# Recutting the column tiles of a decoder trunk, and alternating two PSUM sets in its short convolution

## The chip, the cores and the metric

One Trainium2 chip, all 8 NeuronCores, each with a share of the tokens and all of the weights. The metric is the device time of the slowest core in microseconds (us). A die is four cores (0 to 3, 4 to 7).

The program has two states. In the fast one all cores show the same mean granted TensorE clock and runs agree within 0.3%. In the slow one the cores of one die, or of both, show a lower clock and take longer. A run is called undisturbed below when no die shows a lowered clock.

Words used below: TensorE multiplies a weight block by the columns of the other, the moving operand, and leaves its sums in PSUM; ScalarE and VectorE read PSUM and work on the tiles in SBUF. In the lines of the profile, PE is TensorE and PEld its weight loads, DVE is VectorE, ACT is ScalarE, POOL and SP issue the transfers. L317 is a line of the kernel, x48 a number of instructions, and [1.76 <-DVE ...] the idle time before them and what ended it. A line of the chain or of a timeline begins with start and length in us; a line by windows gives the window, its length, the busy times of PE, PEld, DVE, ACT and POOL (with the number of instructions), the granted clock, the DMA share and GB/s.

## The reference, cut to what matters

A two-layer trunk on a prompt group and a sample group. Each core holds 1024 prompt tokens, 16 sample tokens and, for what has to look back, 128 tokens before its prompt half.

```python
for i in range(2):
    h = h + 0.5 * swiglu(rmsnorm(h), ffn1)      # 2048 -> 5632 -> 2048
    a = rmsnorm(h)
    m = chunk_gmlp(a) if i == 0 else short_conv(a)
    h = h + m
    h = h + 0.5 * swiglu(rmsnorm(h), ffn2)
    h = h + sigmoid(rmsnorm(h) @ w_gate) * (p[i] @ w_proj)
y = rmsnorm(h)

# short_conv: bg, cg, xh = split(a @ w_in, 3);  ci = cg * xh
#             co[t] = w0*ci[t-2] + w1*ci[t-1] + w2*ci[t];  (bg * co) @ w_out
```

The first feed-forward and the v half of the gMLP need all 128 + 1024 + 16 = 1168 columns (tokens). After that the convolution needs only the last two of the 128 tokens before: 2 + 1024 + 16 = 1042 columns.

## The kernel before

Tokens lie along the free dimension: `h`, `xn` and `buf2` are [128, 16, 1168]. A row of `xn` (bf16) is 2336 bytes. The 1024 main columns came first, then the 128 earlier ones, then the 16 samples, so the 1042 needed ones were 0 to 1023 and 1150 to 1167.

```python
TT_FULL = [(0, 512), (512, 512), (1024, 144)]   # (first column, columns)
TT      = [(0, 512), (512, 512), (1150, 18)]

def mm_group(ws, wres, nk, rhs_fn, tts, pset, pres, reads):
    for k in range(nk):                          # weight blocks 128 x 128
        for ti, (t0, tn) in enumerate(tts):      # column tiles, one PSUM bank each
            matmul(pset[ti][:, 0:tn], lhsT=ws[:, k, :], rhs=xn[:, k, t0:t0+tn], ...)
```

Every stage calls `mm_group` for one output chunk after another, into the PSUM sets `PA` and `PB` (three banks each). One weight block is three matmuls; a group with 16 blocks is 48. Weights come in by six slots of 512 KB.

Between stages stands a normalisation:

```python
for (t0, tn) in tts:
    for c in range(16):
        ScalarE: sq[c % 2] = h[:, c, tile] ** 2
        TensorE: pst += ones.T @ sq[c % 2]
    ScalarE: rt = sqrt(pst / D + eps);  VectorE: rstd = 1 / rt
    for c in range(16):
        VectorE: xn[:, c, tile] = h[:, c, tile] * gain[c] * rstd
```

The convolution does three groups for each of its 16 chunks:

```python
for c in range(16):
    group -> PA;  ScalarE: cgs = PA              # cg
    group -> PB;  VectorE: ci = PB * cgs, then co from ci   # xh
    group -> PA;  VectorE: buf2[:, c] = PA * co  # bg
```

Of the kernel before, what the change touches and what calls it, by code (L numbers as in the profile page):

```python
# [6 lines left out]
F32 = mybir.dt.float32  # L7
F32R = mybir.dt.float32r
BF16 = mybir.dt.bfloat16
AF = mybir.ActivationFunctionType  # L10
# [10 lines left out]
TT_FULL = [(0, 512), (512, 512), (1024, 144)]  # L21
TT = [(0, 512), (512, 512), (1150, 18)]
# [102 lines left out]
def build_program():  # L125
# [73 lines left out]
    def sbt(name, shape, dt):  # L199
        uid[0] += 1  # L200
        return nc.sbuf_tensor("%s_u%d" % (name, uid[0]), shape, dt)
# [5 lines left out]
    with contextlib.ExitStack() as es:  # L207
# [70 lines left out]
        with contextlib.ExitStack() as ms:  # L278
# [131 lines left out]
            def ple(l, tts):  # L410
                with contextlib.ExitStack() as ps_:
                    pT = ps_.enter_context(sbt("pT", [128, 2, TH], BF16))
                    pblocks = [(j * 128, 128, j * 128) for j in range(8)] + [(1150, 18, 1150)]
# [36 lines left out]
            def gmlp():  # L450
                rmsnorm(G_MIX + 0, TT_FULL)
                with contextlib.ExitStack() as gs:
# [28 lines left out]
                    for c in range(NCH):  # L481
# [4 lines left out]
                        def emit_v(c=c, pset=pset):  # L486
                            nc.scalar.activation(out=buf2[:, c, 0:512], in_=pset[0][:, 0:512], func=AF.Gelu_apprx_tanh)
                            nc.scalar.activation(out=buf2[:, c, 512:1024], in_=pset[1][:, 0:512], func=AF.Gelu_apprx_tanh)
                            nc.scalar.activation(out=buf2[:, c, 1024:1152], in_=pset[2][:, 0:128], func=AF.Gelu_apprx_tanh)
                            return nc.scalar.activation(out=vsf[:, c, 0:16], in_=pset[2][:, 128:144], func=AF.Gelu_apprx_tanh)  # L490
# [147 lines left out]
            def sconv():  # L638
                rmsnorm(G_MIX + 1, TT)
                with contextlib.ExitStack() as cs:  # L640
# [7 lines left out]
                    co = C(sbt("co", [128, 1024], F32))  # L648
                    cit = C(sbt("cit", [128, NCH, 18], F32))
                    cos = C(sbt("cos", [128, 16], F32))  # L650
                    for c in range(NCH):
                        w0, w1, w2 = gcol(G_WC, c), gcol(G_WC + 1, c), gcol(G_WC + 2, c)
                        ws, wres = wget("c_in", 0, 0, 16, D + c * 128)
                        mm_group(ws, wres, 16, xn_rhs, TT, PA, "psA", XN_ALL)

                        def emit_cg():
                            last = None
                            for ti, (t0, tn) in enumerate(TT):
                                last = nc.scalar.activation(out=cgs[:, t0:t0 + tn], in_=PA[ti][:, 0:tn], func=AF.Copy)
                            return last  # L660
                        S.op("act", ["psA"], ["cgs"], emit_cg)
                        ws, wres = wget("c_in", 0, 0, 16, 2 * D + c * 128)
                        mm_group(ws, wres, 16, xn_rhs, TT, PB, "psB", XN_ALL)
                        cb = cib[c % 2]

                        def emit_ci(cb=cb, c=c):
                            nc.vector.tensor_tensor(out=cb[:, 2:514], in0=PB[0][:, 0:512], in1=cgs[:, 0:512], op=ALU.mult)
                            nc.vector.tensor_tensor(out=cb[:, 514:1026], in0=PB[1][:, 0:512], in1=cgs[:, 512:1024], op=ALU.mult)
                            nc.vector.tensor_tensor(out=cb[:, 0:2], in0=PB[2][:, 0:2], in1=cgs[:, 1150:1152], op=ALU.mult)
                            return nc.vector.tensor_tensor(out=cit[:, c, 2:18], in0=PB[2][:, 2:18], in1=cgs[:, 1152:1168],  # L670
                                                           op=ALU.mult)
                        S.op("dve", ["psB", "cgs"], [("cib", c % 2), ("cit", c)], emit_ci)

                        S.op("dve", [("cib", c % 2)], [("cit", c)], lambda cb=cb, c=c: nc.vector.tensor_copy(
                            out=cit[:, c, 0:2], in_=cb[:, 1024:1026]))
                        S.op("dve", [("cib", c % 2)], ["co"], lambda cb=cb, w0=w0: nc.vector.tensor_scalar(
                            out=co[:], in0=cb[:, 0:1024], scalar1=w0, scalar2=None, op0=ALU.mult))
# [189 lines left out]
```

## Time and profile before

| | before |
|---|---|
| five times before the prediction | 5913, 5916, 6540, 6639, 6785 us (median 6540) |
| profiled run | fast; cores 5907.1 to 5914.6 us, clock 0.939 to 0.941 |
| one weight block, 1168 columns | 494.1 ns (7.91 us a group) |
| one weight block, 1042 columns | 457.1 ns (7.31 us a group) |
| convolution, chunk to chunk | 23.84 us |
| normalisation, first square to first matmul | 46.95 us |

Divide a group's length by its 16 blocks: that is the number that the change is about. The lines themselves are in the prediction.

### The profile page before, as it was taken

The numbers are of one execution on the slowest core, as the hardware profiler recorded it, in microseconds if no ns is written. First come the engines' busy times: TensorE is split into PE (matmuls) and PEld (weight loads), VectorE is DVE, ScalarE is ACT, GpSimd is POOL, SyncE is SP. The second block draws the span as 40 slices with busy tenths as digits, with TensorE's granted clock in tenths as the row PEclk, the third lists the DMA queues.
The fourth block names the chain that finished last, engine by engine and source line by source line (L and its number), as shares of the span: only waits on it lengthen the run. The fifth ranks groups of instructions, "written<-read, shape, count | busy, mean of one in ns | idle before, by whom it ended". The sixth has DMA issues, their size and how long they took to land.

```text
span 5914.6 us, 78413 instructions; the slowest of 8 cores (5907.1 to 5914.6 us)
## 1 busy us (share of the span) xinstructions
PE 5398.7 (91%) x33572; PEld 2668.8 (45%) x33572; DVE 1205.3 (20%) x2549; ACT 542.9 (9%) x1286; POOL 811.3 (14%) x724
## 2 busy tenths in 40 slices
PE   5999999975698999999779999997999899999976
PEld 3555555533344444444334444443444444444434
DVE  3111010124312110101330101113321201010135
ACT  2000000020102000000220000001000200000020
POOL 0111111100011111111111111110111111111110
PEclk7999999976798999999789999997999899999978
DMA  4777777743375777776457787874777577878734
GB/s 90 66 65 68 66 67 67 65 43 29 37 72 48 71 75 72 72 72 66 40 52 73 71 73 70 73 71 46 67 66 65 47 72 72 73 71 72 68 40 93
DMA packets 1405253, 382.73 MB, mean 65 GB/s; under 512 B 1398838, under 2 KB 1402330, under 8 KB 1402526
## 3 DMA queue, kind: packets, MB, share of 16 engines
q0 software_dynamic: 1395968, 354.46, 66.3%
q1 hardware_dynamic: 8942, 23.24, 1.2%
q8 instruction: 270, 4.42, 0.3%
q14 instruction: 73, 0.60, 0.0%
HBM read 723.28 MB, written 8.93 MB: 124 GB/s over the span
## 4 chain that ended last, share of the span: by engine, by line
PE 88%; DVE 7%; ACT 2%; DMA 2%; issue 2%; DVEq 0%; ACTq 0%; SPq 0%
PE pa_u L317 46%; PE pb_u L317 39%; DVE xn_u L350 3%; PE pst_u L340 1%; ACT sq_u L337 1%; DVE rstd_u L347 1%; DMA x_tok_u<-xin 1%; ACT sig_u L426 1%; DVE buf_u L551 1%; DVE st_u L515 0%; DVE fst_u L763 0%; DVE yo_u L777 0%; DMA p_tok_u<-pin 0%; PE x_pt_u L257 0%; DVE vhb_u L528 0%
## 5 line engine op out<-in xcount | busy, mean ns | idle before, releaser
L317 PE MATMUL pa_u<-xn_u,wsl_u 128*128 128x512 bf16 (+2 forms) x12288 | 1961.1, 315 | 119.5 <-DVE xn_u L350 67.4
L317 PE MATMUL pb_u<-xn_u,wsl_u 128*128 128x512 bf16 (+2 forms) x9984 | 1583.2, 314 | 0.0
L317 PEld LDWEIGHTS pa_u<-xn_u,wsl_u 128*128 128x128 bf16 x12288 | 933.3, 97 | 1115.8 <-issue 158.4
L317 PEld LDWEIGHTS pb_u<-xn_u,wsl_u 128*128 128x128 bf16 x9984 | 760.3, 96 | 791.8
L317 PE MATMUL pa_u<-buf_u,wsl_u 128*128 128x512 bf16 (+2 forms) x4992 | 794.1, 314 | 28.9 <-DVE buf_u L398 22.5
L317 PE MATMUL pb_u<-buf_u,wsl_u 128*128 128x512 bf16 (+2 forms) x4992 | 790.2, 313 | 0.0
L398 DVE TENSOR_TENSOR buf_u<-pb_u,sg_u 128x512 bf16<-128x512 f32 x528 | 247.1, 523 | 2396.0 <-PE pb_u L317 2396.0
L317 PEld LDWEIGHTS pa_u<-buf_u,wsl_u 128*128 128x128 bf16 x4992 | 378.4, 97 | 430.2 <-issue 37.8
L317 PEld LDWEIGHTS pb_u<-buf_u,wsl_u 128*128 128x128 bf16 x4992 | 377.3, 96 | 396.2
L389 ACT ACTIVATE sg_u<-pa_u 128x512 f32<-128x512 f32 x528 | 209.5, 469 | 3268.5 <-PE pa_u L317 3268.4
L301 POOL DMA_DIRECT2D wsl_u<-ffn_w_gate x176 | 201.1, 1143 | 1365.5 <-PE pa_u L317 1364.7
L301 POOL DMA_DIRECT2D wsl_u<-ffn_w_down x192 | 221.4, 1153 | 1162.8 <-PE pa_u L317 593.2
L301 POOL DMA_DIRECT2D wsl_u<-ffn_w_up x176 | 201.0, 1142 | 1060.3 <-PE pb_u L317 1060.3
L340 PE MATMUL pst_u<-sq_u,ones_r_u 128*128 128x512 f32 (+2 forms) x384 | 205.1, 615 | 97.2 <-ACT sq_u L337 95.7
L363 DVE SCALAR_TENSOR_TENSOR h_u<-pa_u,h_u 128x512 f32<-128x512 f32 (+2 forms) x288 | 134.8, 523 | 546.9 <-PE pa_u L317 546.9
L363 DVE SCALAR_TENSOR_TENSOR h_u<-pb_u,h_u 128x512 f32<-128x512 f32 (+2 forms) x288 | 134.8, 523 | 522.0 <-PE pb_u L317 522.0
L337 ACT ACTIVATE sq_u<-h_u 128x512 fp32r<-128x512 f32 (+2 forms) x384 | 178.7, 497 | 557.9 <-DVE h_u L360 244.1
L350 DVE SCALAR_TENSOR_TENSOR xn_u<-h_u,colt_u,rstd_u 128x512 bf16<-128x512 f32 (+2 forms) x384 | 194.9, 584 | 2.9 <-DVE rstd_u L347 0.5
L340 PEld LDWEIGHTS pst_u<-sq_u,ones_r_u 128*128 128x128 f32 x384 | 105.0, 285 | 198.2 <-issue 197.7
L301 POOL DMA_DIRECT2D wsl_u<-c_w_in x48 | 54.8, 1142 | 378.3 <-PE pa_u L317 276.5
L301 POOL DMA_DIRECT2D wsl_u<-a_w_in x32 | 36.5, 1142 | 435.2 <-PE pa_u L317 334.8
L436 DVE TENSOR_TENSOR pletmp_u<-pb_u,sig_u 128x512 f32<-128x512 f32 (+1 forms) x96 | 43.9, 512 | 208.7 <-ACT sig_u L426 208.7
(112 smaller groups left out, 1004.0 us busy)
## 6 DMA issues: line engine op xcount, KB each, us to landing
wsl_u<-ffn_w_gate POOLq DMA_DIRECT2D x176, 512.0 KB, 8.2
wsl_u<-ffn_w_up POOLq DMA_DIRECT2D x176, 512.0 KB, 8.2
wsl_u<-ffn_w_down POOLq DMA_DIRECT2D x128, 480.0 KB, 7.9
wsl_u<-ffn_w_down POOLq DMA_DIRECT2D x64, 448.0 KB, 7.1
wsl_u<-c_w_in POOLq DMA_DIRECT2D x48, 512.0 KB, 8.7
wsl_u<-a_w_in POOLq DMA_DIRECT2D x32, 512.0 KB, 7.4
wsl_u<-ple_w_gate POOLq DMA_DIRECT2D x32, 512.0 KB, 8.2
x_tok_u<-xin SPq DMA_DIRECT2D x9, 1024.0 KB, 6.8
```

The lines of the kernel that those rows point to most:

```text
L301: lambda s=s, nk=nk, ent=ent: nc.gpsimd.dma_start(out=wslots[s][:, 0:nk, :], in_=wsrc(ent)))
L317: last = nc.tensor.matmul(pset[ti][:, 0:tn], lhsT=ws[:, k, :], rhs=rhs_fn(k, t0, tn), start=(k == 0), stop=(k == nk - 1))
L337: lambda c=c, t0=t0, tn=tn: nc.scalar.activation(out=sq[c % 2][:, 0:tn], in_=h[:, c, t0:t0 + tn], func=AF.Square))
L340: lambda c=c, tn=tn: nc.tensor.matmul(pst[:, 0:tn], lhsT=ones_r[:], rhs=sq[c % 2][:, 0:tn], start=(c == 0), stop=(c == NCH - 1)))
L347: lambda tn=tn: nc.vector.reciprocal(out=rstd[:, 0:tn], in_=rt[:, 0:tn]))
L350: lambda c=c, t0=t0, tn=tn: nc.vector.scalar_tensor_tensor(out=xn[:, c, t0:t0 + tn], in0=h[:, c, t0:t0 + tn], scalar=gcol(g, c), in1=rstd[ ...
L363: last = nc.vector.scalar_tensor_tensor(out=h[:, d, t0:t0 + tn], in0=pset[ti][:, 0:tn], scalar=scale, in1=h[:, d, t0:t0 + tn], op0=ALU.mul ...
L389: last = nc.scalar.activation(out=sgb[:, t0:t0 + tn], in_=PA[ti][:, 0:tn], func=AF.Silu)
L398: last = nc.vector.tensor_tensor(out=buf2[:, kk, t0:t0 + tn], in0=PB[ti][:, 0:tn], in1=sgb[:, t0:t0 + tn], op=ALU.mult)
L426: last = nc.scalar.activation(out=sb[:, t0:t0 + tn], in_=PA[ti][:, 0:tn], func=AF.Sigmoid)
L436: last = nc.vector.tensor_tensor(out=tmp[:, t0:t0 + tn], in0=PB[ti][:, 0:tn], in1=sb[:, t0:t0 + tn], op=ALU.mult)
L551: last = nc.vector.scalar_tensor_tensor(out=buf2[:, c, c0:c0 + 128], in0=pset[i // 4][:, (i % 4) * 128:(i % 4 + 1) * 128], scalar=gcol(G_L ...
```

## The change

Its intent: no narrow matmul any more, and no wait between the convolution's chunks. The 128 earlier tokens move to the front, so that the 1042 columns are one run (126 to 1167) and can be cut into three even tiles.

```diff
-TT_FULL = [(0, 512), (512, 512), (1024, 144)]
-TT = [(0, 512), (512, 512), (1150, 18)]
+TT_FULL = [(0, 392), (392, 392), (784, 384)]
+TT = [(126, 346), (472, 352), (824, 344)]
 ...
-pblocks = [(j * 128, 128, j * 128) for j in range(8)] + [(1150, 18, 1150)]
+pblocks = [(j * 128, 128, j * 128) for j in range(9)] + [(1152, 16, 1152)]
 ...  # convolution
+if c % 2 == 0:
+    PX, pxr, PY, pyr = PA, "psA", PB, "psB"
+else:
+    PX, pxr, PY, pyr = PB, "psB", PA, "psA"
-mm_group(ws, wres, 16, xn_rhs, TT, PA, "psA", XN_ALL)      # cg
+mm_group(ws, wres, 16, xn_rhs, TT, PX, pxr, XN_ALL)
-mm_group(ws, wres, 16, xn_rhs, TT, PB, "psB", XN_ALL)      # xh
+mm_group(ws, wres, 16, xn_rhs, TT, PY, pyr, XN_ALL)
-mm_group(ws, wres, 16, xn_rhs, TT, PA, "psA", XN_ALL)      # bg
+mm_group(ws, wres, 16, xn_rhs, TT, PX, pxr, XN_ALL)
 ...  # co and cos become one tile coe [128, 1042]; the elementwise loops run over TT;
 ...  # the host puts the 128 earlier tokens at rows 0..127 and the main ones at 128..1151
```

More of the change, by code (lines that the diff above doesn't have):

```diff
@@ L20 @@
 NSAMP = 16
-TT_FULL = [(0, 512), (512, 512), (1024, 144)]
-TT = [(0, 512), (512, 512), (1150, 18)]
+TT_FULL = [(0, 392), (392, 392), (784, 384)]
+TT = [(126, 346), (472, 352), (824, 344)]
+C_MAIN = 128
+C_SAMP = 1152
 PIECES = [(0, 15), (15, 30), (30, 44)]
@@ L486, in emit_v @@
                         def emit_v(c=c, pset=pset):
-                            nc.scalar.activation(out=buf2[:, c, 0:512], in_=pset[0][:, 0:512], func=AF.Gelu_apprx_tanh)
-                            nc.scalar.activation(out=buf2[:, c, 512:1024], in_=pset[1][:, 0:512], func=AF.Gelu_apprx_tanh)
-                            nc.scalar.activation(out=buf2[:, c, 1024:1152], in_=pset[2][:, 0:128], func=AF.Gelu_apprx_tanh)
-                            return nc.scalar.activation(out=vsf[:, c, 0:16], in_=pset[2][:, 128:144], func=AF.Gelu_apprx_tanh)
+                            for ti, (t0, tn) in enumerate(TT_FULL):
+                                nc.scalar.activation(out=buf2[:, c, t0:t0 + tn], in_=pset[ti][:, 0:tn],
+                                                     func=AF.Gelu_apprx_tanh)
+                            tn = TT_FULL[2][1]
+                            return nc.scalar.activation(out=vsf[:, c, 0:16], in_=pset[2][:, tn - 16:tn],
+                                                        func=AF.Gelu_apprx_tanh)
                         S.op("act", [pres], [("b2", c), ("vsf", c)], emit_v)
@@ L647, in sconv @@
                     cib = [C(sbt("cib%d" % i, [128, 1026], F32)) for i in range(2)]
-                    co = C(sbt("co", [128, 1024], F32))
+                    coe = C(sbt("coe", [128, 1042], F32))
                     cit = C(sbt("cit", [128, NCH, 18], F32))
-                    cos = C(sbt("cos", [128, 16], F32))
                     for c in range(NCH):
                         w0, w1, w2 = gcol(G_WC, c), gcol(G_WC + 1, c), gcol(G_WC + 2, c)
+                        if c % 2 == 0:
+                            PX, pxr, PY, pyr = PA, "psA", PB, "psB"
+                        else:
+                            PX, pxr, PY, pyr = PB, "psB", PA, "psA"
@@ L653, in sconv, with emit_cg @@
                         ws, wres = wget("c_in", 0, 0, 16, D + c * 128)
-                        mm_group(ws, wres, 16, xn_rhs, TT, PA, "psA", XN_ALL)
-                        def emit_cg():
+                        mm_group(ws, wres, 16, xn_rhs, TT, PX, pxr, XN_ALL)
+                        def emit_cg(PX=PX):
                             last = None
                             for ti, (t0, tn) in enumerate(TT):
-                                last = nc.scalar.activation(out=cgs[:, t0:t0 + tn], in_=PA[ti][:, 0:tn], func=AF.Copy)
+                                last = nc.scalar.activation(out=cgs[:, t0:t0 + tn], in_=PX[ti][:, 0:tn], func=AF.Copy)
@@ L660, in emit_cg @@
                             return last
-                        S.op("act", ["psA"], ["cgs"], emit_cg)
+                        S.op("act", [pxr], ["cgs"], emit_cg)
                         ws, wres = wget("c_in", 0, 0, 16, 2 * D + c * 128)
-                        mm_group(ws, wres, 16, xn_rhs, TT, PB, "psB", XN_ALL)
+                        mm_group(ws, wres, 16, xn_rhs, TT, PY, pyr, XN_ALL)
                         cb = cib[c % 2]
-                        def emit_ci(cb=cb, c=c):
-                            nc.vector.tensor_tensor(out=cb[:, 2:514], in0=PB[0][:, 0:512], in1=cgs[:, 0:512], op=ALU.mult)
-                            nc.vector.tensor_tensor(out=cb[:, 514:1026], in0=PB[1][:, 0:512], in1=cgs[:, 512:1024], op=ALU.mult)
-                            nc.vector.tensor_tensor(out=cb[:, 0:2], in0=PB[2][:, 0:2], in1=cgs[:, 1150:1152], op=ALU.mult)
-                            return nc.vector.tensor_tensor(out=cit[:, c, 2:18], in0=PB[2][:, 2:18], in1=cgs[:, 1152:1168],
-                                                           op=ALU.mult)
@@ L672, in sconv @@
-                        S.op("dve", ["psB", "cgs"], [("cib", c % 2), ("cit", c)], emit_ci)
-                        S.op("dve", [("cib", c % 2)], [("cit", c)], lambda cb=cb, c=c: nc.vector.tensor_copy(
-                            out=cit[:, c, 0:2], in_=cb[:, 1024:1026]))
-                        S.op("dve", [("cib", c % 2)], ["co"], lambda cb=cb, w0=w0: nc.vector.tensor_scalar(
-                            out=co[:], in0=cb[:, 0:1024], scalar1=w0, scalar2=None, op0=ALU.mult))
-                        S.op("dve", [("cib", c % 2), "co"], ["co"], lambda cb=cb, w1=w1: nc.vector.scalar_tensor_tensor(
-                            out=co[:], in0=cb[:, 1:1025], scalar=w1, in1=co[:], op0=ALU.mult, op1=ALU.add))
@@ L680, in sconv @@
-                        S.op("dve", [("cib", c % 2), "co"], ["co"], lambda cb=cb, w2=w2: nc.vector.scalar_tensor_tensor(
-                            out=co[:], in0=cb[:, 2:1026], scalar=w2, in1=co[:], op0=ALU.mult, op1=ALU.add))
-                        S.op("dve", [("stT", k) for k in range(32)], ["cos"], lambda c=c, w0=w0: nc.vector.tensor_scalar(
-                            out=cos[:], in0=stT[:, c, :], scalar1=w0, scalar2=None, op0=ALU.mult))
-                        S.op("dve", ["cos"], ["cos"], lambda c=c, w1=w1: nc.vector.scalar_tensor_tensor(
-                            out=cos[:], in0=stT[:, 16 + c, :], scalar=w1, in1=cos[:], op0=ALU.mult, op1=ALU.add))
@@ L687, in sconv @@
-                        S.op("dve", ["cos", ("cit", c)], ["cos"], lambda c=c, w2=w2: nc.vector.scalar_tensor_tensor(
-                            out=cos[:], in0=cit[:, c, 2:18], scalar=w2, in1=cos[:], op0=ALU.mult, op1=ALU.add))
-                        ws, wres = wget("c_in", 0, 0, 16, c * 128)
-                        mm_group(ws, wres, 16, xn_rhs, TT, PA, "psA", XN_ALL)
-                        def emit_yc(cb=cb, c=c):
-                            nc.vector.tensor_tensor(out=buf2[:, c, 0:512], in0=PA[0][:, 0:512], in1=co[:, 0:512], op=ALU.mult)
-                            nc.vector.tensor_tensor(out=buf2[:, c, 512:1024], in0=PA[1][:, 0:512], in1=co[:, 512:1024],
-                                                    op=ALU.mult)
-                            nc.vector.tensor_tensor(out=buf2[:, c, 1150:1152], in0=PA[2][:, 0:2], in1=cb[:, 0:2], op=ALU.mult)
-                            return nc.vector.tensor_tensor(out=buf2[:, c, 1152:1168], in0=PA[2][:, 2:18], in1=cos[:],
-                                                           op=ALU.mult)
@@ L699, in sconv, with emit_ci @@
-                        S.op("dve", ["psA", "co", "cos", ("cib", c % 2)], [("b2", c)], emit_yc)
+                        def emit_ci(cb=cb, c=c, PY=PY):
+                            last = None
+                            for ti, (t0, tn) in enumerate(TT):
+                                nm = min(t0 + tn, C_SAMP) - t0
+                                last = nc.vector.tensor_tensor(out=cb[:, t0 - 126:t0 - 126 + nm], in0=PY[ti][:, 0:nm],
+                                                               in1=cgs[:, t0:t0 + nm], op=ALU.mult)
+                                if nm < tn:
+                                    last = nc.vector.tensor_tensor(out=cit[:, c, 2:18], in0=PY[ti][:, nm:tn],
+                                                                   in1=cgs[:, C_SAMP:C_SAMP + 16], op=ALU.mult)
+                            return last
@@ new lines, in sconv, with emit_cp @@
+                        S.op("dve", [pyr, "cgs"], [("cib", c % 2), ("cit", c)], emit_ci)
+                        def emit_cp(cb=cb, c=c):
+                            nc.vector.tensor_copy(out=cit[:, c, 0:2], in_=cb[:, 1024:1026])
+                            nc.vector.tensor_copy(out=coe[:, 0:2], in_=cb[:, 0:2])
+                            nc.vector.tensor_scalar(out=coe[:, 1026:1042], in0=stT[:, c, :], scalar1=w0, scalar2=None,
+                                                    op0=ALU.mult)
+                            return nc.vector.tensor_scalar(out=coe[:, 2:1026], in0=cb[:, 0:1024], scalar1=w0, scalar2=None,
+                                                           op0=ALU.mult)
@@ new lines, in sconv, with emit_c1 @@
+                        S.op("dve", [("cib", c % 2)] + [("stT", k) for k in range(32)], ["coe", ("cit", c)], emit_cp)
+                        def emit_c1(cb=cb, c=c):
+                            nc.vector.scalar_tensor_tensor(out=coe[:, 1026:1042], in0=stT[:, 16 + c, :], scalar=w1,
+                                                           in1=coe[:, 1026:1042], op0=ALU.mult, op1=ALU.add)
+                            return nc.vector.scalar_tensor_tensor(out=coe[:, 2:1026], in0=cb[:, 1:1025], scalar=w1,
+                                                                  in1=coe[:, 2:1026], op0=ALU.mult, op1=ALU.add)
@@ new lines, in sconv, with emit_c2 @@
+                        S.op("dve", [("cib", c % 2), "coe"], ["coe"], emit_c1)
+                        def emit_c2(cb=cb, c=c):
+                            nc.vector.scalar_tensor_tensor(out=coe[:, 1026:1042], in0=cit[:, c, 2:18], scalar=w2,
+                                                           in1=coe[:, 1026:1042], op0=ALU.mult, op1=ALU.add)
+                            return nc.vector.scalar_tensor_tensor(out=coe[:, 2:1026], in0=cb[:, 2:1026], scalar=w2,
+                                                                  in1=coe[:, 2:1026], op0=ALU.mult, op1=ALU.add)
@@ new lines, in sconv, with emit_yc @@
+                        S.op("dve", [("cib", c % 2), ("cit", c), "coe"], ["coe"], emit_c2)
+                        ws, wres = wget("c_in", 0, 0, 16, c * 128)
+                        mm_group(ws, wres, 16, xn_rhs, TT, PX, pxr, XN_ALL)
+                        def emit_yc(c=c, PX=PX):
+                            last = None
+                            for ti, (t0, tn) in enumerate(TT):
+                                last = nc.vector.tensor_tensor(out=buf2[:, c, t0:t0 + tn], in0=PX[ti][:, 0:tn],
+                                                               in1=coe[:, t0 - 126:t0 - 126 + tn], op=ALU.mult)
+                            return last
@@ L700, in sconv @@
+                        S.op("dve", [pxr, "coe"], [("b2", c)], emit_yc)
                     with contextlib.ExitStack() as c2:
@@ L746, in build_program @@
                 out=gfb[:], in_=bass.AP(final_norm.tensor, 0, [[0, 128], [1, D]])))
-            fblocks = [(j * 128, 128, j * 128, 0) for j in range(8)] + [(1150, 18, 1024, 2)]
+            fblocks = [(C_MAIN + j * 128, 128, j * 128, 0) for j in range(8)] + [(C_SAMP, 16, 1024, 0)]
             for bi, (c0, n, row0, skip) in enumerate(fblocks):
@@ L836 @@
         pin = np.zeros((2, TH, DPLE), np.float32)
-        xin[0:1024] = x_prompt[b, half * 1024:(half + 1) * 1024]
-        pin[:, 0:1024] = p_prompt[:, b, half * 1024:(half + 1) * 1024]
+        xin[128:1152] = x_prompt[b, half * 1024:(half + 1) * 1024]
+        pin[:, 128:1152] = p_prompt[:, b, half * 1024:(half + 1) * 1024]
         if half == 1:
-            xin[1024:1152] = x_prompt[b, 896:1024]
-            pin[:, 1024:1152] = p_prompt[:, b, 896:1024]
+            xin[0:128] = x_prompt[b, 896:1024]
+            pin[:, 0:128] = p_prompt[:, b, 896:1024]
         xin[1152:1168] = x_sample[c * 16:(c + 1) * 16, 0]
```

## The prediction

> **What bounds the kernel now.** First the view of the cores: all eight spans lie between 5907.1 and 5914.6 us at a mean granted clock of 0.939 to 0.941, so the profiled run is an undisturbed (fast) one and core 5, the slowest, speaks for all. The five times before are 5913, 5916, 6540, 6639 and 6785 us: two fast runs and three slow ones. I predict the fast state only, against 5914.6; a median that falls among slow runs says how often the slow state came, not what the change does.
>
> Then the page's chain that ended last:
>
> ```profile
> PE 88%; DVE 7%; ACT 2%; DMA 2%; issue 2%; DVEq 0%; ACTq 0%; SPq 0%
> ```
>
> TensorE is 88% of the path and no wait for a weight transfer is in it. So what matters is what one matmul group costs. The chain in order of time shows two group lengths, first in a stage that works on all 1168 columns, then in one on 1042:
>
> ```profile
> 141.88 7.91 PE pb_u L317 x48
> 149.79 7.91 PE pa_u L317 x48
> ...
> 1837.77 7.31 PE pb_u L317 x48
> 1845.09 7.31 PE pa_u L317 x48
> ```
>
> Both are 48 matmuls (16 weight blocks times 3 column tiles). The view by windows says at what clock:
>
> ```profile
> 500.00:720.00 220.00, 220.00 (x1337) 114.95 (x1336) 21.04 (x42) 17.74 (x42) 32.16 (x28) 1.00 0.75 66
> 2170.00:2370.00 200.00, 200.00 (x1315) 95.63 (x1314) 19.20 (x42) 15.27 (x41) 31.48 (x28) 1.00 0.76 71
> ```
>
> TensorE is never idle in either stretch, the granted clock is 1.00, and the DMA engines are 75 and 76% busy. Per weight block: 7.906/16 = 494.1 ns for 512+512+144 columns, and 7.313/16 = 457.1 ns for 512+512+18. So 126 columns fewer save only 37.0 ns, 0.29 ns a column. That is the slack that the change aims at. The groups by shape give the number of narrow matmuls:
>
> ```profile
> L317 PE MATMUL pa_u<-xn_u,wsl_u 128*128 128x18 bf16 x3264 | 564.2, 173 | 0.0
> L317 PE MATMUL pb_u<-xn_u,wsl_u 128*128 128x18 bf16 x2496 | 430.2, 172 | 0.0
> L317 PE MATMUL pa_u<-buf_u,wsl_u 128*128 128x18 bf16 x1312 | 226.3, 172 | 0.0
> L317 PE MATMUL pb_u<-buf_u,wsl_u 128*128 128x18 bf16 x1312 | 226.0, 172 | 0.0
> ```
>
> Their means (172 ns) are latencies with overlap, not costs; the counts matter: 8384, plus 64 on the embedding tile.
>
> Last, the waits of TensorE. One repeats in the short-convolution stage, and the timeline shows it:
>
> ```profile
> PE pa_u L317 <- DVE buf_u L697: 26.7, 15, 2.1
> ```
>
> ```profile
> 4122.65 0.17 DVE L697 TENSOR_TENSOR buf_u<-pa_u,cos_u 128x16 bf16<-128x16 f32 x1
> 4122.94 7.20 PEld L317 LDWEIGHTS pa_u<-xn_u,wsl_u 128*128 128x128 bf16 x48 [2.02 <-issue]
> 4122.97 7.46 PE L317 MATMUL pa_u<-xn_u,wsl_u 128*128 128x512 bf16 x48 [1.76 <-DVE buf_u L697]
> ```
>
> Each of the 16 chunks uses the PSUM sets A, B, A, and the next begins with A again: its first group has to wait until VectorE has read the previous chunk's last one.
>
> **What the Trainium skill says.** (1) "TensorE: Matmul & The Clock Gate", section "Back-to-back issue gap": an isolated warm matmul costs N/2.4 + 2.5 ns, and up to 64 columns it costs about 60 cycles, 25 ns, however narrow. The trace agrees: 1168/2.4 + 3 x 2.5 = 494.2 against 494.1, and taking two 512-column matmuls (2 x 215.8) off 457.1 leaves 25.4 ns for the 18-column one. The same section's lower "sustained" figure of 131 ns at N=512 does not fit this trace. (2) "Perfetto Trace Analysis", section "Matmuls": independent groups should rotate through PSUM banks so that evacuation of one overlaps the next group. The A, B, A, A order breaks this once per chunk, and the 1.76 us is the price. (3) "SBUF — State Buffer", section "Operand start alignment": an operand may start at any multiple of its element size, but this is "about legality, not speed". The new tiles start at columns 126, 472 and 824 (byte 252, 944, 1648); no run here shows yet whether wide matmuls stream at full rate from there.
>
> **The change part by part.**
>
> *1042-column groups, retiled to 346+352+344.* Same 1042 columns, same 48 matmuls and weight loads per group, but none under the floor. New block: 1042/2.4 + 3 x 2.5 = 441.7 ns; old 457.1; saved 15.4 ns, or 7.31 to 7.07 us a group. All of it is on the path where groups follow each other. Counting blocks: gMLP second half and output 512, three feed-forwards 3 x 2112 = 6336, embedding gates 2 x 256 = 512, convolution input and output 1024; sum 8384. 8384 x 15.4 ns = **-129 us**. The 64 projection blocks gain nothing: there TensorE waits for the sigmoid's PSUM read anyway (20.8 us over 30 waits).
>
> *1168-column groups, retiled to 392+392+384.* 1168/2.4 + 3 x 2.5 either way: 144 columns (62.5 ns) were already above the floor. **0 us.** The chain has 7.91 us here before and must have it after.
>
> *PSUM rotation in the convolution.* The first matmul of one chunk to that of the next is 4146.81 - 4122.97 = 23.84 us; three groups are 21.94. So 1.90 us a chunk is stall and handover; with the sets alternating A,B,A then B,A,B each set's reader has a whole group's time (7.07 us) to finish. VectorE's work per chunk (the rows of its timeline added up) is some 7.5 us of the new 21.2, so it does not become the bound. 15 x 1.9 = **-28 us**.
>
> *VectorE's convolution code.* Two small multiplies a chunk go (the 2-column ones, 0.15 us each), a 2-column copy comes, samples and main part share a tile. It lies beside the matmuls. **0 us.**
>
> *Normalisations with 1042 columns (six).* Each is a gap of TensorE: in the one after the gMLP, 46.95 us from the first square (1781.67) to the first matmul (1828.62). VectorE sets the end there: reciprocal 3.35 and 16 multiplies 10.69 us for each wide tile, then 0.27 + 2.45 for the 18 columns. Equal tiles change which engine paces. From the rows: the square-matmul pair takes 0.818 us per chunk at 512 columns, 0.51 at 144 and 0.41 at 18, so 0.39 + 0.83 ns x N, 0.68 us at 346. VectorE per tile: 16 x (0.135 + 1.04 ns x N) = 7.9 us, reciprocal 2.3, some 10.4 with gaps. Squares per tile: 16 x 0.68 + 1.05 = 12.0 us, so now the squares pace it. First tile 14.7 - 2.2 = 12.5; two more, 24.0; then root 0.5, VectorE's last tile 10.3: 47.3 us, 0.4 more than before. The short last tile had hidden behind VectorE's work; now its successor is exposed, but the first tile starts sooner. **+2 us** for six; the same sum gives 0 for the two with 1168 columns.
>
> *Embedding load (two).* Nine full blocks and one of 16 rows instead of eight and one of 18. The last blocks come about 1.6 us apart (2812.0, 2813.8, 2815.0, 2816.9), nothing runs beside them. **+3 us.**
>
> *The rest.* Final stage, gMLP mixing (nine blocks), input load: same instructions within two columns. **0.** Cold first groups of a stage (9 to 10 us instead of 7.3) stay.
>
> Sum: -129 - 28 + 2 + 3 = -152; I take 2 us back for cold blocks, where a narrow matmul at half clock wastes less. 5914.6 - 150 = **5765 us**, 2.5% less.
>
> **The rivals.**
>
> A. *Start addresses cost TensorE something.* If reading from byte 252 cost 5 ns a matmul, three in 8384 blocks would be +126 us and nearly all of part one would be gone: 5890. For it: no wide matmul has been seen at such a start. Against: rows of the tile are 2336 bytes apart, so the starts of the 512-column tiles already vary by 32 bytes from row to row, and every group took 7.31. I give it 6%.
>
> B. *Weights become the bound.* Shorter groups ask for 512 KB each 7.07 us, so DMA goes from 0.76 to some 0.79. Against: no TensorE wait for weights before, six slots, 8.2 us to landing against about 40 us of lead; the down-projections already run at 0.79. If it came, the 1042-column groups would gain half: 5830. 4%.
>
> C. *Power.* TensorE gets denser; the granted clock could fall, and the whole be nothing or worse. Against: the 1168-column stages are as dense (486.7 of 494.1 ns) as the others will be (434.2 of 441.7) and had clock 1.00. 2% for the fast state.
>
> D. *Normalisations lose more than computed,* because squares pace them: at +3 us each, 24 us in all, the time is 5785. It moves the number, hardly the verdict.
>
> **Range and chances.** The large term rests on a linear law that fits two stages to 0.1 ns, so I give it +-8 us; the convolution +-4, normalisations and loads +-10, run-to-run 0.3% or 15. Together about 20: 5740 to 5795. The 2% line is 5796. Faster 0.88, within 2% 0.11 (A, B, or D with bad luck), slower 0.01.
>
> **What would show it.** Groups of 7.07 us in the 1042-column stages (A: longer, with clock 1.00; C: clock below 1; B: TensorE waits for the weight tiles); 7.91 us unchanged in the others; no TensorE wait behind the convolution's last multiply and 21.2 us from chunk to chunk; normalisation gaps of 47 us, with VectorE now idle between tiles; 1.5 us more before the embedding's squares. If the groups are not 7.07 us, the prediction is wrong at its root.

## The result, and the profile after

| | before | changed |
|---|---|---|
| all runs, median | 6392.7 us (18 runs) | 5994.1 us (10 runs) |
| runs below 5950 us | 5912 to 5916 (6 of 18) | 5763 to 5766 (4 of 10), and 5816 |
| the others | 6156 to 6930 | 6172 to 6777 |
| ratio of fast runs | | 0.9765, 95% interval 0.9729 to 0.9801 |

The ratio is the mean time of one kernel's fast runs over that of the other's of the same rounds, so not quite the ratio of any two medians. Its interval reaches past 0.98, so by the 2% line the verdict is "unclear". The wide interval goes back to one run above all: 5816 us counts as fast although die 0 was at clock 0.927 to 0.933 in it. The four undisturbed runs, 5763 to 5766, over the 5912 to 5916 of before make 0.975. The profiled run (5762.8 us) is one of these:

```profile
core 1: 5761.8 us, clock 0.936
core 5: 5757.9 us, clock 0.937
```

The chain in order of time, in a feed-forward with 1042 columns, has the groups that the arithmetic wanted, where the kernel before has 7.31 (start, length, what):

```profile
2150.69 7.07 PE pb_u L319 x48
2157.76 7.07 PE pa_u L319 x48
```

Windows in a 1168-column and in a 1042-column stage:

```profile
500.00:720.00 220.00, 220.00 (x1338) 130.65 (x1337) 21.06 (x42) 17.76 (x42) 32.12 (x28) 1.00 0.75 67
2150.00:2350.00 200.00, 200.00 (x1360) 132.92 (x1359) 19.22 (x42) 17.45 (x45) 33.05 (x29) 1.00 0.78 74
```

TensorE is never idle, its clock is 1.00, and the weights ask the DMA engines for 0.78 instead of 0.76. In 1168-column stages the groups are still 7.91 us.

In the convolution the timeline has no wait in front of a group any more; the third line below is the multiply that reads the last group of a chunk, and the next chunk's groups start 7.07 us apart right through it:

```profile
4061.03 7.23 PE L319 MATMUL pb_u<-xn_u,wsl_u 128*128 128x346 bf16 x48
4068.10 7.23 PE L319 MATMUL pa_u<-xn_u,wsl_u 128*128 128x346 bf16 x48
4068.44 1.37 DVE L713 TENSOR_TENSOR buf_u<-pb_u,coe_u 128x346 bf16<-128x346 f32 x3 [1.42 <-PE pb_u L319]
4075.17 7.23 PE L319 MATMUL pb_u<-xn_u,wsl_u 128*128 128x346 bf16 x48
```

The normalisation after the gMLP took 46.95 us from first square to first matmul before, 1781.67 to 1828.62:

```profile
1781.67 1.15 ACT L337 ACTIVATE sq_u<-h_u 128x512 fp32r<-128x512 f32 x2 [120.53 <-DVE h_u L360]
...
1811.30 3.35 DVE L347 RECIPROCAL rstd_u<-rt_u 128x512 f32<-128x512 f32 x1
...
1825.55 0.27 DVE L347 RECIPROCAL rstd_u<-rt_u 128x18 f32<-128x18 f32 x1
...
1828.62 1.89 PE L317 MATMUL pa_u<-xn_u,wsl_u 128*128 128x512 bf16 x5 [11.01 <-DVE xn_u L350]
```

Now it takes 47.10, 1773.97 to 1821.07:

```profile
1773.97 0.87 ACT L339 ACTIVATE sq_u<-h_u 128x346 fp32r<-128x346 f32 x2 [119.52 <-DVE h_u L362]
...
1798.89 2.35 DVE L349 RECIPROCAL rstd_u<-rt_u 128x352 f32<-128x352 f32 x1 [1.47 <-ACT rt_u L346]
...
1810.52 2.30 DVE L349 RECIPROCAL rstd_u<-rt_u 128x344 f32<-128x344 f32 x1 [1.15 <-ACT rt_u L346]
...
1821.07 3.35 PE L319 MATMUL pa_u<-xn_u,wsl_u 128*128 128x346 bf16 x11 [11.33 <-DVE xn_u L352]
```

VectorE now waits 1.47 and 1.15 us for the root before its second and third tile; before, it went from tile to tile without a gap (no idle time stands behind its two reciprocals above). So the squares have become the pace, and the total is nearly the same.

### The profile page after: what moved, and what is told of

Same layout as the page of the kernel before. It is cut to its first block, busy times and chain, and to the rows that moved or that the text cites. A ratio compares the mean times of both kernels' runs of the same rounds, so it can differ in the third digit from the quotient of the medians.

```text
span 5761.8 us, 78422 instructions; the slowest of 8 cores (5755.1 to 5761.8 us)
## 1 busy us (share of the span) xinstructions
PE 5265.9 (91%) x33576; PEld 3390.6 (59%) x33576; DVE 1203.4 (21%) x2551; ACT 538.3 (9%) x1286; POOL 811.2 (14%) x724
## 4 chain that ended last, share of the span: by engine, by line
PE 89%; DVE 5%; ACT 3%; issue 2%; DMA 2%; ACTq 0%; DVEq 0%; SPq 0%
PE pa_u L319 45%; PE pb_u L319 40%; PE pst_u L342 2%; ACT sq_u L339 2%; DVE xn_u L352 1%; DMA x_tok_u<-xin 1%; ACT sig_u L428 1%; DVE buf_u L555 1%; DVE st_u L519 0%; DVE fst_u L780 0%; DMA p_tok_u<-pin 0%; DVE yo_u L794 0%; DVE rstd_u L349 0%; PE x_pt_u L259 0%; DVE vhb_u L532 0%
## 5 line engine op out<-in xcount | busy, mean ns | idle before, releaser
L319 PE MATMUL pa_u<-xn_u,wsl_u 128*128 128x344 bf16 (+4 forms) x11904 | 1857.2, 316 | 95.0 <-DVE xn_u L352 68.9
L319 PEld LDWEIGHTS pa_u<-xn_u,wsl_u 128*128 128x128 bf16 x11904 | 1169.4, 98 | 748.5 <-issue 112.8
L319 PE MATMUL pb_u<-xn_u,wsl_u 128*128 128x352 bf16 (+4 forms) x10368 | 1605.3, 315 | 0.0
L319 PEld LDWEIGHTS pb_u<-xn_u,wsl_u 128*128 128x128 bf16 x10368 | 1014.5, 98 | 555.6
L319 PE MATMUL pa_u<-buf_u,wsl_u 128*128 128x344 bf16 (+4 forms) x4992 | 779.5, 316 | 29.3 <-DVE buf_u L400 22.9
L319 PE MATMUL pb_u<-buf_u,wsl_u 128*128 128x344 bf16 (+4 forms) x4992 | 771.7, 314 | 0.0
L400 DVE TENSOR_TENSOR buf_u<-pb_u,sg_u 128x346 bf16<-128x346 f32 (+1 forms) x528 | 247.3, 524 | 2332.3 <-PE pb_u L319 2332.3
L391 ACT ACTIVATE sg_u<-pa_u 128x346 f32<-128x346 f32 (+1 forms) x528 | 209.4, 469 | 3185.2 <-PE pa_u L319 3185.2
L342 PE MATMUL pst_u<-sq_u,ones_r_u 128*128 128x352 f32 (+4 forms) x384 | 198.9, 612 | 101.8 <-ACT sq_u L339 101.0
L352 DVE SCALAR_TENSOR_TENSOR xn_u<-h_u,colt_u,rstd_u 128x352 bf16<-128x352 f32 (+4 forms) x384 | 194.9, 585 | 2.9 <-DVE rstd_u L349 0.5
L303 POOL DMA_DIRECT2D wsl_u<-ple_w_gate x32 | 37.4, 1168 | 347.9 <-PE pa_u L319 347.9
```

The costliest lines, as they stand in the source:

```text
L303: lambda s=s, nk=nk, ent=ent: nc.gpsimd.dma_start(out=wslots[s][:, 0:nk, :], in_=wsrc(ent)))
L319: last = nc.tensor.matmul(pset[ti][:, 0:tn], lhsT=ws[:, k, :], rhs=rhs_fn(k, t0, tn), start=(k == 0), stop=(k == nk - 1))
L342: lambda c=c, tn=tn: nc.tensor.matmul(pst[:, 0:tn], lhsT=ones_r[:], rhs=sq[c % 2][:, 0:tn], start=(c == 0), stop=(c == NCH - 1)))
L352: lambda c=c, t0=t0, tn=tn: nc.vector.scalar_tensor_tensor(out=xn[:, c, t0:t0 + tn], in0=h[:, c, t0:t0 + tn], scalar=gcol(g, c), in1=rstd[ ...
L391: last = nc.scalar.activation(out=sgb[:, t0:t0 + tn], in_=PA[ti][:, 0:tn], func=AF.Silu)
L400: last = nc.vector.tensor_tensor(out=buf2[:, kk, t0:t0 + tn], in0=PB[ti][:, 0:tn], in1=sgb[:, t0:t0 + tn], op=ALU.mult)
```

## The experiments

All are edits of the changed kernel unless it is said otherwise, and all gave right results. Only fast runs, or the undisturbed die of a slow one, are used for lengths.

**1. The wide cut back.**

```diff
-TT = [(126, 346), (472, 352), (824, 344)]
+TT = [(126, 512), (638, 512), (1150, 18)]
```

> The changed kernel with only its 1042-column tiles put back to 512+512+18, at the new places (columns 126, 638, 1150); rotation and layout stay. Theory (a narrow matmul costs 25 ns however narrow): groups of 7.31 us again, 8384 blocks x 15.4 ns = +129 us, less some 2 us in the normalisations; a fast run 5889 us, 0.996 of before. Rival (the start of the tiles at an odd byte costs TensorE time, or the even split gains by something other than the floor): groups longer than 7.31 us, since two 512-column tiles now start at bytes 252 and 1276; at 5 ns a matmul 7.39 to 7.55 us and a fast run of 5930 us or more. What slow runs show is not used.

Measured: undisturbed runs 5937 to 5940 us, above the kernel before (fast runs of 5914 to 5923) although the rotation is in. The ratio is 1.0053, with a fast run of 5969 us in it whose die 1 was at clock 0.934. The chain:

```profile
2170.19 7.40 PE pa_u L319 x48
2177.59 7.40 PE pb_u L319 x48
```

7.40 us, not 7.31: 462.5 ns a block, 5.4 more than the same three widths took at their old places. This is on the side of the rival: something about where the tiles lie costs time, though the even tiles from the same column 126 do not pay it.

**2. Just above the floor.**

```diff
+TT = [(126, 512), (638, 466), (1104, 64)]
```

> The changed kernel with 1042 columns cut as 512+466+64, as uneven as before in all but one respect: the narrow tile is at 64 columns, 64/2.4 + 2.5 = 29.2 ns, just above the 25.4 ns that an 18-column one took. Theory (a floor): groups of 7.07 us as with even tiles, a fast run within 10 us of 5762. Rival 1 (a fixed extra of a narrow matmul, 25.4 - 10.0 = 15.4 ns whatever its width below some 100 columns): groups of 7.31 us, 5890 us. Rival 2 (the weight load of the next matmul, recorded at 96 to 98 ns, must hide behind the one before): a narrow tile of 29 ns exposes much of it, groups of 7.3 us or more.

Measured: 7.10 us a group, 5780 to 5781 us, ratio 0.9769. A narrow tile of 64 columns does not bring back the 15 ns a block that the 18-column one cost, and exposes no weight load, so rivals 1 and 2 fall. But the fast runs are 17 us above 5763, outside the 10 that I had allowed, and 7.10 is 2.1 ns a block more than the columns make.

**3. Without the rotation.**

```diff
-                        if c % 2 == 0:
+                        if True:
```

> The changed kernel with the convolution's PSUM sets back in the order A, B, A in every chunk; tiles as changed. Theory (the next chunk's first group waits for the last reader of set A): the wait of TensorE for the convolution's last multiply is back, 15 times 1.8 us, 21.2 + 1.9 = 23.1 us from chunk to chunk, a fast run 5762 + 28 = 5790 us. Rival (the even tiles have shortened VectorE's last multiply or its path enough that the order no longer matters): 5762 us.

Measured: 5792 us undisturbed, 29 us more than the change (ratio to before 0.9789, by the 2% line "unclear"). The wait is back (us in total, times, longest):

```profile
PE pa_u L319 <- DVE buf_u L713: 25.4, 15, 1.7
```

From chunk to chunk 4074.22 to 4097.27, 23.05 us. The theory holds to a microsecond.

**4. Four tiles for the squares.**

```diff
-sq = [... for i in range(2)]      # sq[c % 2]
+sq = [... for i in range(4)]      # sq[c % 4]
```

> The changed kernel with four tiles instead of two for the squares of the normalisations. Theory (with even tiles the exchange of two square tiles between ScalarE and TensorE paces a normalisation, 0.68 us a chunk, and VectorE waits some 1.2 to 1.5 us before each tile): the squares run at 0.45 us a chunk or so, VectorE paces again, a normalisation goes from 47.1 to about 41 us, eight of them save about 50 us, a fast run 5712 us. Rival (the clock of TensorE, not the number of tiles, sets the 0.68 us): no more than 10 us saved, 5755 us.

The profiled run was slow, on die 0 only; the cores of the other die took 5701.8 to 5709.5 us, and one run of the eight was 5712.5. On core 6 the normalisation takes 1762.02 to 1802.29, 40.3 us, and the 16 squares of its first tile 6.21 us, 0.39 a chunk. The clock was not the limit: the exchange of two tiles was.

This run also shows what the slow state is. The two dies in the same execution, and then the same two windows on core 0 (slow die) and on core 6:

```profile
die 0 (median of its cores): 5982.1 us, clock 0.896
die 1 (median of its cores): 5707.9 us, clock 0.945
```

```profile
500.00:720.00 220.00, 220.00 (x1118) 120.53 (x1117) 22.55 (x45) 11.41 (x27) 27.45 (x24) 0.82 0.61 56
2150.00:2350.00 200.00, 198.20 (x1347) 131.56 (x1346) 26.06 (x57) 11.64 (x30) 33.87 (x29) 1.00 0.91 74
```

```profile
500.00:720.00 220.00, 220.00 (x1337) 130.71 (x1336) 20.28 (x41) 17.75 (x42) 31.77 (x28) 1.00 0.70 67
2150.00:2350.00 200.00, 198.13 (x1346) 131.51 (x1345) 20.56 (x45) 15.12 (x39) 32.31 (x28) 1.00 0.77 73
```

TensorE is busy without a break in the first window on both, but it gets through 1118 matmuls instead of 1337 on the slow die, 0.84, at a granted clock of 0.82; in the second window both are at 1.00. In this run the slow state is a stretch, not the whole run.

**5. A table of cuts in one kernel.** The gate and up groups of the three 1042-column feed-forwards use another cut every three hidden chunks (six groups).

```diff
+    ct = CUTS[f // 3] if tts is TT else tts
-    mm_group(ws, wres, 16, xn_rhs, tts, PA, "psA", XN_ALL)
+    mm_group(ws, wres, 16, xn_rhs, ct, PA, "psA", XN_ALL)
```

> A table of 14 ways to cut the columns in one kernel: in the gate and up groups of the three feed-forwards with 1042 columns, three hidden chunks each (six groups) use one cut, the rest is the changed kernel; the result stays right (some cuts compute a few columns too many). The length of a group is read from the chain in order of time where the clock is 1.00. The runs before showed 7.40 us for 512+512+18 where the kernel before has 7.31, and 7.10 us for 512+466+64 where the floor alone gives 7.07: 5.4 and 2.1 ns a block too much. Theory A (the start of a wide tile that is no multiple of 32 bytes costs TensorE 2.7 ns): wide starts at 224 or 192 bytes give 7.31 us (512+512+32 and 512+512+48 alike, under the floor), starts at 252, 248, 244, 240 or 250 bytes 7.40, and 512+402+128 from byte 252 shows it too, 7.15 us. Theory B (the extra belongs to the narrow tile and what follows it, and comes only with a wide tile at such a start): 512+402+128 from byte 252 is 7.07 us, and 18 first then 512+512 at multiples of 32 bytes is 7.31. Theory C (a narrow tile's own start decides): 512+502+42 from byte 224 with the narrow tile at byte 2252 is 7.40. The floor itself: 512+480+64 from byte 224 (1056 columns) gives 1056/2.4 + 7.5 = 447.5 ns a block, 7.16 us, with no extra.

Die 1 was a little disturbed (clock 0.931 to 0.936), so core 0 is read. The timeline, where the start of one group to that of the next is its length: the wide cut from byte 252 (7.40), then 512+512+32 from byte 224 (7.31), then 512+402+128 from byte 252 (7.10):

```profile
1884.35 7.55 PE L336 MATMUL pb_u<-xn_u,wsl_u 128*128 128x512 bf16 x47
1891.75 7.55 PE L336 MATMUL pa_u<-xn_u,wsl_u 128*128 128x512 bf16 x47
...
1921.17 7.46 PE L336 MATMUL pa_u<-xn_u,wsl_u 128*128 128x512 bf16 x47
1928.48 7.46 PE L336 MATMUL pb_u<-xn_u,wsl_u 128*128 128x512 bf16 x47
...
2204.64 7.26 PE L336 MATMUL pa_u<-xn_u,wsl_u 128*128 128x512 bf16 x47
2211.74 7.26 PE L336 MATMUL pb_u<-xn_u,wsl_u 128*128 128x512 bf16 x47
```

Starts at 192, 224 and 240 bytes give 7.31 with narrow tiles of 48, 32 and 24 columns: all the same, so it is a floor. 512+480+64 from byte 224 gives 7.16, with nothing extra. Starts at 244, 248, 250 and 252 give 7.39 to 7.42. So the grid is 16 bytes, not the 32 of theory A. 512+402+128 shows 2.1 ns (theory B wanted 0, theory A 5.4), 498+512+32 from byte 252 shows none, and the narrow tile at byte 2252 shows 1.6 (theory C wanted 5). None of the three survives whole.

**6. The kernel before with four square tiles.** The same edit as in 4, on the kernel before.

> The kernel before with four tiles for the squares instead of two. Theory (there VectorE sets the end of a normalisation, and only the first tile's squares stand before it): only the first tile gains, 16 x some 0.3 us = 4 to 5 us a normalisation, and the changed kernel's gain from the same edit (47.1 to 40.3 us) is larger; eight normalisations, a fast run 5877 us, 36 us less than before. Rival (the exchange of squares paces both kernels alike): 50 us or more.

Measured: 5877 to 5880 us undisturbed; the normalisation takes 42.7 us instead of 46.95. Against the undisturbed runs of before in the same rounds, 5910 to 5915, it gains 34 us where the changed kernel gains 52. (The ratio of fast runs, 0.9914, is "unclear": two runs of before with a disturbed die, 5980 and 5987 us, count as fast.) All of the gain of a normalisation lies in front of the first reciprocal, which now comes 11.1 us after the first square instead of 15.4. So the squares paced only the first tile before and pace all three now: the reading of the normalisation is shown.

**7. Four square tiles on the changed kernel again.**

> The changed kernel with four tiles for the squares again, since its profile and all but one of its runs fell in the slow state: a fast run 5712 us, ratio to before 0.966, normalisations of 40.3 us as its undisturbed die showed.

Measured: one undisturbed run, 5711.3 us, all cores at clock 0.944 to 0.947, the rest slow. With the 5712.5 of experiment 4 that is two undisturbed runs within 1.2 us, about 0.966 of before; with one fast run in each set no interval was given. Undisturbed, this version beats both kernels.

**8. Where the extra starts.** A second table: one tile of 504 to 512 columns first, then 400, then 130 to 138.

> A second table of cuts in the same places as the first, to find where the extra of a wide tile begins: one wide tile first (its start and width varied), then 400 columns and a rest of 130 to 138, so that neither is wide nor under the floor. The first table gave: 512 columns from byte 252 cost 2.1 ns more than N/2.4 + 2.5 (7.10 us a group), 498 from the same byte and 512 from byte 240 nothing. Theory A (a tile whose columns touch more than 64 pieces of 16 bytes pays about 2 ns): from byte 252 the widths 512, 510, 508 give 7.10 us and 506, 504 give 7.07; from byte 248, 512 and 510 give 7.11 and 508 gives 7.08; from byte 244, 512 gives 7.13 and 510 gives 7.09; from byte 250, 512 gives 7.11 and 507 gives 7.07; 512 from byte 240 gives 7.11 with nothing extra in it (1048 columns). Theory B (only a full tile of 512 columns pays, off 16 bytes): every width below 512 is free, 510 and 508 from byte 252 at 7.07. Theory C (any tile over some 500 columns off 16 bytes pays): 506 and 504 from byte 252 at 7.10 too.

Read on core 0 (the undisturbed die, 5774.1 us at 0.938). From byte 252, groups of 508 (two lines) and 506 columns, then of 504:

```profile
1966.73 7.30 PE L336 MATMUL pb_u<-xn_u,wsl_u 128*128 128x508 bf16 x48
1973.88 7.30 PE L336 MATMUL pa_u<-xn_u,wsl_u 128*128 128x508 bf16 x48
...
2002.29 7.23 PE L336 MATMUL pa_u<-xn_u,wsl_u 128*128 128x506 bf16 x48
2009.36 7.23 PE L336 MATMUL pb_u<-xn_u,wsl_u 128*128 128x506 bf16 x48
...
2160.00 7.32 PE L336 MATMUL pb_u<-xn_u,wsl_u 128*128 128x504 bf16 x48
2167.16 7.32 PE L336 MATMUL pa_u<-xn_u,wsl_u 128*128 128x504 bf16 x48
```

508 takes 7.14, 506 takes 7.07 and 504 takes 7.16. No theory of the tile's width can do that. But 506 is the one width here whose next tiles begin at 126 + 506 = 632 and at 1032, multiples of 8 columns, 16 bytes. The same holds down the table: 508 from byte 248 and 510 from byte 244 end at column 632 too and pay nothing, 512 from either pays. What counts is whether the *cuts inside the row* lie on 16 bytes. The start of the first tile alone costs nothing (7.07 from byte 252), except 1.2 ns at byte 250. In blocks without a narrow tile, two cuts off 16 bytes cost 4.5 to 5.8 ns (7.4 from byte 250); one cut off and one on, as in experiment 2 (bytes 1276 and 2208), costs 2.1. So all three theories fell, and the rule tested next was formed from the two tables.

**9. The changed kernel again.**

> The changed kernel itself once more, on the chip and in the hour of the table: an undisturbed run 5763 us against 5914 of before (ratio 0.9745); some runs of both kernels in the slow state, and in those at least one die with a lower granted clock in the records, the other die, if undisturbed, at 5755 to 5762 us. Rival: the change alters what an undisturbed run takes from chip to chip, and the 0.9765 of the first comparison is real: 5775 us.

Measured: 5762.4 us undisturbed against 5911 to 5917 of before, 0.9745 if the two are taken alone. Only one run was undisturbed on both dies, a second counts as fast (5813 us, one die at 0.928), four were slow, so no interval was given. In the slow ones the cores of the other die stayed at 5753 to 5765 us. In the same rounds 9 of 11 runs of before were fast. Chance or not, this is too few to say that the change brings more slow runs.

**10. Even tiles, cuts off 16 bytes.**

```diff
+TT = [(126, 348), (474, 352), (826, 342)]
```

> The changed kernel with its three even tiles moved by two columns: 348+352+342 from columns 126, 474 and 826. The two cuts inside the row then fall at bytes 948 and 1652, no multiples of 16, where the change has 944 and 1648, which are. The two tables leave one rule standing: a block of three tiles takes the longer of N/2.4 + 7.5 ns and 3.33 ns for each piece of 16 bytes that its tiles touch (a piece that two tiles share counts twice) + 4.2 ns. The change touches 44+44+43 = 131 pieces, 440.9 ns, so the columns rule, 441.7; these tiles touch 45+45+43 = 133, 447.5 ns, 7.16 us a group, 8384 x 5.8 = 49 us more than the change, a fast run 5811 us. Rival (what the tables showed needs a tile near 512 columns or a narrow one): 7.07 us and 5763 us.

Measured: 7.14 us a group, 5796 and 5798 us, 34 us more than the change.

```profile
2159.48 7.14 PE pa_u L319 x48
2166.62 7.14 PE pb_u L319 x48
```

The rival falls: even tiles pay too. Moved by two columns, the change would have lost a quarter of what the recut brings. The size is 4.6 ns, not 5.8; the rule of the pieces has the place right and the amount only roughly. (8384 x 4.6 ns would be 38 us; the 4 us between were not followed. The ratio to before, 0.9804, is "unclear" by the 2% line.)

**11. The wide cut with both cuts on 16 bytes.**

```diff
+TT = [(126, 506), (632, 512), (1144, 24)]
```

> The changed kernel with its 1042 columns cut as wide as before, but with both cuts at multiples of 16 bytes: 506+512+24 from columns 126, 632 and 1144 (bytes 1264 and 2288). The rule of the pieces gives nothing extra here, so the first experiment's 7.40 us should fall to what the floor alone makes: 506/2.4 + 2.5 = 213.3, 512: 215.8, narrow 25.4, sum 454.6 ns, 7.27 us a group; 8384 x 12.9 = 108 us more than the change, less 2 in the normalisations, a fast run 5869 us. Rival (any narrow last tile after a start at byte 252 costs the extra): 7.36 us, 5917 us or more.

Measured: 7.27 us and 5870.1 and 5870.9 us, within 2 us of what was expected. So the floor alone makes 107 us here, and the 5937 of experiment 1 is the floor plus the two cuts off the grid.

```profile
2171.70 7.27 PE pa_u L319 x48
2178.96 7.27 PE pb_u L319 x48
```

## Why the prediction was right or wrong

**The range was wrong.** It held 5740 to 5795, and the median of the ten runs is 5994. The step that failed is the first paragraph's choice, "I predict the fast state only", and with it one term of the range, "run-to-run 0.3% or 15": it leaves the state out. Measured, the median of the ten runs lies 230 us above the undisturbed runs (5994 against 5764), and even within the fast runs the spread is 53 us (5816 against 5763). The mechanism, and with it what an undisturbed run takes, was right: 5763 to 5766 against 5765. But five of ten runs were slow, and a median over such a mix lies wherever the mix puts it. The kernel before shows it without any change: its medians in the five sets of runs are 6392.7, 5918.7, 6241.4, 5912.7 and 6610.7 us, although the fastest run of each set took 5910 to 5914. The five times before the prediction, three of them slow, said so already. A range for the median of a mixed sample would have had to reach from 5740 to beyond 6400.

**The chance of "faster" was too high for the same reason.** One run with a partly disturbed die, 0.9% above the others where the prediction allowed 0.3%, entered the fast mean and moved the ratio from 0.975 to 0.9765. Faster by 2.35%, with an interval that reaches past 2%, is unclear.

**The parts, by the terms of the sum:**

- *1042-column groups, -129 us.* Held: 7.07 us. Experiment 11 scales: 107 us for 12.9 ns a block, so 15.4 ns are 128.
- *1168-column groups, 0.* Held: 7.91 us before and after.
- *Rotation, -28.* Held: 29 us in experiment 3, chunk to chunk 21.2 us after.
- *Normalisations, +2.* The mechanism held, the size was smaller: from first square to first matmul the six went from 46.95, 47.75, 47.54, 57.95, 45.50 and 47.51 us to 47.10, 47.48, 47.27, 58.44, 45.85 and 47.23, together +0.2. The one taken apart is paced by the squares as computed. Experiments 4 and 6 show the pace.
- *Embedding load, +3.* Held in sum, 2.5 us: from the first load's issue to the first square 16.7 us (2764.17 to 2780.91) against 15.0 (2803.39 to 2818.39) the first time, 15.9 (5486.93 to 5502.84) against 15.1 (5635.67 to 5650.75) the second.
- *Cold blocks, +2.* Not taken apart.

The span went from 5914.6 to 5761.8, 152.8 us, of which the input load, which the change doesn't touch, gave 2.9 (the first square came at 80.03 us instead of 82.95). That was lucky and is not explained. What is left, 149.9 us, is so near to the 150 because small misses cancel: the convolution stage, from its first group to the next square, went from 518.0 to 472.1 us, 45.9 where 43.8 were computed, the normalisations cost 2 less, and the gMLP's second half gained 4.8 us (1540.00 to 1781.67 before, 1537.07 to 1773.97 after) instead of some 8. Behind a 3.2 us gap of TensorE there, a window over the gap and the group behind it shows clock 0.79 (1647 to 1663 us), where the kernel before has 1.00 (1653 to 1667 us); whether the change or chance does that is not shown.

**The rivals.** B and C did not come in fast runs (clock 1.00 in the stage above, no wait for weights), nor did D: the normalisations cost 0.2 us more, not 24 (its 5785 is a slip besides; 5765 - 2 + 24 is 5787). A, at 6%, is real but elsewhere than I put it: cuts off 16 bytes cost 4.6 ns a block in experiment 10. The change escapes it because 472 and 824 are multiples of 8; nothing in the prediction asks for that, so it was luck. My argument against A, that starts already vary by 32 bytes from row to row, could not have seen a grid of 16.

What stays open: why a cut off 16 bytes costs time. That TensorE reads the moving operand in pieces of 16 bytes and reads a shared piece twice fits the lengths of blocks without a narrow tile within 1.3 ns, but not the odd start at byte 250 (2.0 ns more). Where the floor already sets the block the rule, as it stands in experiment 10, gives nothing extra, yet 512+512+18 to 22 with both cuts off 16 bytes took 4.9 to 5.4 ns more (6.6 from byte 250), and 512+502+42 with one such cut 1.6. No run shows the reading itself, and none parts the end of one tile from the start of the next by a gap, so which of the two costs is open. What brings a die into the slow state is open too, and whether the change alters how often.

## What to carry to other kernels

Divide a group's length by its weight blocks and compare that with columns/2.4 + 2.5 ns, summed over the block's matmuls: matmuls of 18 to 48 columns cost 25 ns here whatever their width (by the formula, an estimate, the floor ends at 55 columns), so cut the columns evenly, and put the cuts of a bf16 moving operand on multiples of 8 columns where its rows are multiples of 16 bytes, as they are here. Alternate PSUM sets so that no group follows the reader of its own set. And where runs fall in two states, say which number is predicted, the fast run or the median, and give the median the width of the mix.

## What the Trainium skill lacked or had wrong

- "TensorE: Matmul & The Clock Gate", "Back-to-back issue gap", and "SBUF — State Buffer", "Operand start alignment" (which says that it is about legality, not speed): neither has a cost for cuts of a moving operand off 16 bytes. The second page's "Specifications (TRN2)" do name 16-byte cachelines and a penalty for each cross to a new line, the same 16 bytes as the grid here, but no figure and no word of matmul operands; no run here shows that this is the cause. Two such cuts in a block of three bf16 matmuls took a block from 441.7 to 446.2 ns (7.07 to 7.14 us a group).
- "TensorE: Matmul & The Clock Gate", "Back-to-back issue gap", gives one cost, about 60 cycles, for 1 to 64 columns. Here 18 to 48 columns cost 25 ns, but 64 columns 29.2 (7.16 us for 512+480+64: 447.5 - 215.8 - 202.5), as its formula N/2.4 + 2.5 says. Its "sustained" 131 ns at N=512 did not appear; 215.8, by the same formula, fits the blocks of 494.1 and 457.1 ns.
- The same page, Part 1, "Seeing it yourself", tells all-core kernels to budget a 13/16 clock, held while the load lasts, once three cores of a die run dense matmuls. Here, in a fast run (5763 us), all eight cores show clock 1.00 over 920 us on end (1840 to 2760) with TensorE 99% busy; the mean of the run is lower, 0.936 to 0.938, through stretches such as 1265 to 1480 us (0.77 to 0.78, TensorE busy for some 141 of 215 us). A slow die showed 0.82, near the 13/16, in one window and 1.00 in another of the same run. The page makes the limit depend on the data; no page says why executions of one kernel differ.
